# A two-layer hybrid decoder trunk whose instruction order is worked out against another machine model

## The chip, the core and the metric

The kernel runs on one core of a Trainium2 chip. The core has a matrix engine (PE, with its weight loads listed apart as PEld), a vector engine (DVE), a scalar engine (ACT), a general-purpose engine (POOL), a sync engine (SP) that here only issues transfers, and 16 DMA engines that move data between main memory and the on-chip memory. Each engine works through its own instruction list strictly in the order in which the program holds it, and waits on semaphores for the others. The metric is the device time of one execution in microseconds (us); less is better.

## What is computed

Two layers over x of 1024 tokens by 1024 channels, float32. Each layer has a mixer and an MLP, each between two norms:

```python
for l in range(2):
    z = rms_norm(x, g_pre_mix) @ w_in          # columns of three head groups
    # mLSTM, 4 heads of 64, chunks of 128, after a causal convolution and silu
    # sliding-window attention, 8 query heads on 2 key heads of 64, window 128, sinks
    # differential attention, 4 heads, 2 x 32 wide queries and keys, full causal
    x = x + rms_norm(concat(out_m, out_s, out_d) @ w_out, g_post_mix)
    u = square(relu(rms_norm(x, g_pre_mlp) @ w_up))     # 4096 wide
    x = x + rms_norm(u @ w_down, g_post_mlp)
```

## The kernel before, in words

All big products keep nearly float32 precision by splitting each operand into a high and a low part and adding three products: high by high, high by low, low by high. `load_w` (L103 to L118) brings a weight block in chunks by a DMA on SP's queue (L109) and splits it with one ACT and one DVE instruction per piece; `split` (L93, L94) does the same for activations.

A layer runs through these steps, written one after the other in the program:

- `p_d` (in `proj_tiles`, matmuls at L285, PSUM tile `pt`): the projections of the differential attention's queries and keys, with rotary embedding on DVE, stored to main memory as `d_rope` (L318, SP's queue). `p_g2` (L356, tile `pg`): gates and values.
- `e_diff`: the differential attention, 16 steps, each in four parts. `diff_load` loads `ks` and `qs` (L452 to L465, SP's queue). `diff1` makes a score tile `sp` per chunk (L493), reduces it on DVE with the mask (L496), takes the exponential on ACT (L499) and joins the two maps. `diff2` transposes (L520, tile `trd`), splits and multiplies with the values (L528, tile `pv`). `diff3` and `diff4` normalise and transpose back (L538, L555), and the result goes to main memory as `mix_d` (L558).
- `p_s`, `p_m` (L285, `pt`) and `p_g1` (L356, `pn`): the projections of the other two head groups. The key and query parts go to main memory as `s_ropek` (stores at L336) and `s_ropeq` (L318). The order is `p_s`, `p_g1`, `p_m` in layer 0 and `p_m`, `p_s`, `p_g1` in layer 1.
- `e_swa` and `e_mlstm`, interleaved by `run`: window attention (scores at L611, tile `ss`) and the mLSTM recurrence (L762 to L815).
- `out_group`, twice (L848, tile `po`), the second with `post_mix`: output projection, norm, residual, and the transpose for the MLP (L173, tile `tr`).
- The MLP: eight rounds of `up` (L1012, tile `pu`) and `down_mm` (L1057, tile `pd`), the last with `post_mlp`.

The program text is not the order of execution. Every instruction gets a priority number as it is written down, counting up. `ahead(n)` lowers the numbers inside its block by n, so that what stands there counts as that much earlier: `EARLY` (100000) for evacuations of `out_group` and `g2`, 5000 for the first loads, 1000 for weight loads and evacuations of projections, 300 or 200 for the window attention. When the `TileContext` block closes (L1198), the library's scheduler plays the program through on a model of the core. Whenever the model lets an engine take an instruction, the scheduler hands it the one with the lowest number among those whose inputs, by the model's clock, are finished and whose output buffer is free. The order so found is what each engine's list holds, DMA issues on SP's, ACT's and POOL's queues too. Buffers are handed out on the way: a pool has a fixed count per tag, for instance two PSUM buffers for each of the tags `mm`, `ad` and `as`, four of `e` and two of `at` on chip. Semaphore waits are added afterwards and keep the result right under any order. On the chip nothing is reordered: an instruction that is not ready holds up all that stand behind it on its engine. (Only weight loads run beside the matmul ahead of them, as the column PEld of the profile shows.)

The score tiles `sp` of the differential attention take their PSUM buffers from the tag `ad` (`diff1` calls with k of 0 or 1); the transposes and later parts of the first 11 steps take theirs from `as`:

```python
def dtag(k, h, g):
    return "as" if h * 4 + g < 11 and k >= 2 else "ad"
```

## Time and profile before

| | |
|---|---|
| Median of 3 runs | 2559.37 us (2557.65 to 2565.87) |
| The profiled execution, its own time | 2563.38 us |
| Its span, first to last instruction | 2561.6 us |
| Mean granted PE clock | 0.972 |
| Instructions | 32491 |
| Moved by DMA | 227.42 MB, 89 GB/s over the span |
| Matmul lines L1012 and L1057 (MLP) | 25.6% and 24.9% of the chain that ended last |

How to read the profile: busy time is the time in which an engine has an instruction recorded; the "granted clock" is the share of full speed that PE was given; a row of a list of groups names the line, engine, tile and shape, the count, the busy time, the mean duration of one, and the idle time of the engine just before them with what ended it. In a timeline a row is one instruction, or several alike in a run, with its start and its length; matmuls overlap in the records, so the distance from start to start is the pace, not the length. "SPq" is a DMA issue on SP's queue. The chain of waits goes back from the last instruction, at each step to what released it.

### The profile page before, as it was taken

The numbers are of one execution on the slowest core, as the hardware profiler recorded it, in microseconds if no ns is written. First come the engines' busy times: TensorE is split into PE (matmuls) and PEld (weight loads), VectorE is DVE, ScalarE is ACT, GpSimd is POOL, SyncE is SP. The second block draws the span as 40 slices with busy tenths as digits, with TensorE's granted clock in tenths as the row PEclk, the third lists the DMA queues.
The fourth block names the chain that finished last, engine by engine and source line by source line (L and its number), as shares of the span: only waits on it lengthen the run. The fifth ranks groups of instructions, "written<-read, shape, count | busy, mean of one in ns | idle before, by whom it ended". The sixth has DMA issues, their size and how long they took to land.

```text
span 2561.6 us, 32491 instructions
## 1 busy us (share of the span) xinstructions
PE 2397.5 (94%) x11556; PEld 1991.8 (78%) x11556; DVE 1457.8 (57%) x3604; ACT 1076.1 (42%) x2657; POOL 90.8 (4%) x174
## 2 busy tenths in 40 slices
PE   8888989889999999999999998878899999999998
PEld 7767867667888888888778777867678888888887
DVE  6676888775234434443675876867742344334436
ACT  4244777656313312331433645756553123213312
POOL 0000000010000000000000000000100000000000
PEclk9998999999999999999999989989999999999999
DMA  5444354333012101110442334433321112112204
GB/s 169 146 141 132 92 125 121 100 103 107 25 41 66 59 24 50 66 50 25 173 163 86 117 126 132 137 87 106 113 90 41 34 58 66 32 36 66 66 22 160
DMA packets 146002, 227.42 MB, mean 89 GB/s; under 512 B 22512, under 2 KB 60592, under 8 KB 145840
## 3 DMA queue, kind: packets, MB, share of 16 engines
q1 hardware_dynamic: 143680, 221.70, 28.1%
q10 hardware_dynamic: 2160, 3.65, 0.4%
q8 instruction: 91, 1.49, 0.2%
q14 instruction: 71, 0.58, 0.1%
HBM read 179.09 MB, written 46.20 MB: 88 GB/s over the span
## 4 chain that ended last, share of the span: by engine, by line
PE 73%; DMA 11%; DVE 7%; ACT 4%; issue 2%; POOL 1%; SPq 1%; DVEq 0%; POOLq 0%; ACTq 0%
PE pu L1012 26%; PE pd L1057 25%; PE pt L285 7%; PE po L848 2%; PE pg L356 2%; PE pn L356 2%; POOL rs L153 1%; DMA mb<-m_rows 1%; DMA qs<-d_rope 1%; PE pv L528 1%; DMA mix_d<-oo 1%; PE sp L493 1%; DMA mxl<-mix_d 1%; DMA rw<-in_w_t_dram 1%; PE ss L611 1%
## 5 line engine op out<-in xcount | busy, mean ns | idle before, releaser
L1012 PE MATMUL pu<-h2T,wu 128*128 128x512 f32 x3072 | 703.6, 390 | 0.1
L1012 PEld LDWEIGHTS pu<-h2T,wu 128*128 128x128 f32 x3072 | 577.4, 188 | 121.2 <-DVE h2T L94 1.1
L1057 PE MATMUL pd<-wdh,u 128*128 128x512 f32 x2048 | 635.2, 390 | 1.1 <-DVE acm L1068 1.1
L1057 PEld LDWEIGHTS pd<-wdh,u 128*128 128x128 f32 x2048 | 384.8, 188 | 81.1 <-DVE acm L1068 1.5
L1057 PE MATMUL pd<-wdl,u 128*128 128x512 f32 x1024 | 399.0, 390 | 0.0
L1068 DVE TENSOR_TENSOR acm<-acm,pd 128x512 f32<-128x512 f32 x224 | 153.1, 686 | 309.1 <-PE pd L1057 309.0
L1015 ACT ACTIVATE r<-pu 128x512 f32<-128x512 f32 x128 | 75.2, 588 | 537.9 <-PE pu L1012 537.9
L285 PE MATMUL pt<-hT,wt 128*128 128x512 f32 x832 | 287.2, 411 | 2.7 <-DVE lamp L228 1.5
L116 ACT ACTIVATE wu<-rw,gk 128x128 fp32r<-128x128 f32 x512 | 160.2, 390 | 184.7 <-PE pu L1012 132.3
L117 DVE SCALAR_TENSOR_TENSOR wu<-rw,gk,wu 128x128 fp32r<-128x128 f32 x512 | 154.2, 351 | 140.9 <-ACT wu L116 140.8
L1057 PEld LDWEIGHTS pd<-wdl,u 128*128 128x128 f32 x1024 | 192.6, 188 | 39.8
L1018 DVE TENSOR_TENSOR r<-r 128x512 f32<-128x512 f32 x128 | 88.4, 690 | 222.5 <-ACT u L1017 222.5
L285 PEld LDWEIGHTS pt<-hT,wt 128*128 128x128 f32 x832 | 160.5, 196 | 33.6 <-issue 2.3
L285 PE MATMUL pt<-lT,wt 128*128 128x512 f32 x416 | 170.2, 409 | 0.0
L153 POOL TENSOR_TENSOR rs<-ms,mhalf 128x1 f32<-128x1 f32 (+2 forms) x112 | 78.9, 709 | 2351.8 <-DVE ms L151 2283.2
L94 DVE TENSOR_TENSOR wdl<-rw,wdh 128x512 fp32r<-128x512 f32 x128 | 88.5, 692 | 105.1 <-ACT wdh L93 105.0
L848 PE MATMUL po<-woh,mxl 128*128 128x512 f32 x384 | 135.1, 410 | 10.4 <-DVE acc L856 7.8
L93 ACT CAST wdh<-rw 128x512 fp32r<-128x512 f32 x128 | 79.3, 620 | 129.2 <-DMA rw<-in_w_down_dram 129.2
L499 ACT ACTIVATE e<-e,nb 128x256 f32<-128x256 f32 (+7 forms) x128 | 99.4, 777 | 52.4 <-DVE nb L496 47.1
L493 PE MATMUL sp<-ks,qs 96*128 96x512 f32 (+2 forms) x192 | 74.0, 396 | 41.0 <-DMA qs<-d_rope 17.0
L356 PE MATMUL pn<-wv,hT 128*128 128x256 f32 x512 | 110.0, 296 | 0.2 <-ACT mv L707 0.2
L496 DVE CUSTOM_DVE_ANT_0 e<-sp,mdif 128x512 f32<-128x512 f32 (+3 forms) x128 | 74.5, 585 | 33.1 <-PE sp L493 24.0
(225 smaller groups left out, 3361.0 us busy)
## 6 DMA issues: line engine op xcount, KB each, us to landing
rw<-in_w_up_dram SPq DMA_DIRECT2D x128, 256.0 KB
rw<-in_w_down_dram SPq DMA_DIRECT2D x128, 256.0 KB
rw<-in_w_t_dram SPq DMA_DIRECT2D x52, 256.0 KB
tab<-in_rope_dram SPq DMA_DIRECT2D x20, 512.0 KB
xt<-in_x_dram SPq DMA_DIRECT2D x16, 512.0 KB
d_rope<-rot SPq DMA_DIRECT2D x32, 256.0 KB
s_ropeq<-rot SPq DMA_DIRECT2D x32, 256.0 KB
qq<-s_ropeq SPq DMA_DIRECT2D x16, 512.0 KB
```

The lines of the kernel that those rows point to most:

```text
L94: nc.vector.tensor_sub(lo, src, hi.bitcast(F32))
L116: nc.scalar.activation(hi[:, cs], rj, AF.Copy, scale=g)
L117: nc.vector.scalar_tensor_tensor(out=lo[:, cs], in0=rj, scalar=g, in1=hi[:, cs].bitcast(F32), op0=ALU.mult, op1=ALU.subtract)
L153: nc.gpsimd.tensor_tensor(out=rs, in0=ms, in1=mhalf[:, 0:n], op=ALU.pow)
L285: nc.tensor.matmul(q, lhsT=a, rhs=b, start=n == 0, stop=n == 23)
L356: nc.tensor.matmul(q[:, 0:n], lhsT=a, rhs=b, start=i == 0, stop=i == 23)
L493: nc.tensor.matmul(sp[:, 0:w], lhsT=qs[0:96, m, (q % 4) * P:(q % 4 + 1) * P], rhs=ks[m][0:96, c0:c0 + w], start=True, stop=True)
L499: nc.scalar.activation(e[:, 0:L], e[:, 0:L], AF.Exp, bias=nb[:, nch - 1:nch], scale=-1.0, accum_out=den[:, m:m + 1])
L848: nc.tensor.matmul(q, lhsT=mx[:, a, k], rhs=wo[k][b][:, n * 512:(n + 1) * 512], start=i == 0, stop=i == 3 * nk - 1)
L1012: nc.tensor.matmul(q, lhsT=w[:, a, kc], rhs=h2[b + half][:, :, kc], start=n == 0, stop=n == 23)
L1057: nc.tensor.matmul(q, lhsT=U[f][a][:, t * P:(t + 1) * P], rhs=D[f][b][:, n * 512:(n + 1) * 512], start=i == 0, stop=i == 3 * nf - 1)
L1068: nc.vector.tensor_add(a, a, q)
```

## The change

One argument is added where the kernel opens the `TileContext`. The scheduler then plays the program through on the library's detailed simulator of the core in place of its usual, simpler one. The priority numbers, the pools, the instructions and what they compute are the same; what can come out differently is the order of the instructions on each engine, DMA issues among them, and which instance of a pool's buffers a tile gets.

```diff
-    with tile.TileContext(nc) as tc:
+    with tile.TileContext(nc, schedule_with_timeline_sim=True) as tc:
         hybrid_kernel(tc, *args)
```

## The prediction

> **What bounds the kernel now.** I read the page first, then busy time by stretches, the chain of waits, PE's own waits, and last the timeline of one stall.

> ```profile
> span 2561.6 us, 32491 instructions
> PE 2397.5 (94%) x11556; PEld 1991.8 (78%) x11556; DVE 1457.8 (57%) x3604; ACT 1076.1 (42%) x2657; POOL 90.8 (4%) x174
> PE   8888989889999999999999998878899999999998
> PEclk9998999999999999999999989989999999999999
> ```

> PE is busy for 94% of the span, but the digits show that it isn't so evenly. Cutting the span where the chain shows the first and last unbroken MLP matmuls gives five stretches (columns: length; busy time of PE, PEld, DVE, ACT, POOL, each with its count; granted clock; DMA share; GB/s):

> ```profile
> 0.00:593.53 593.53, 512.13 (x2755) 427.28 (x2755) 429.75 (x1221) 336.65 (x868) 41.05 (x81) 0.94 0.43 126
> 593.53:1216.08 622.55, 622.55 (x2741) 515.22 (x2742) 253.57 (x505) 181.06 (x423) 0.00 (x0) 1.00 0.15 49
> 1216.08:1867.36 651.28, 576.18 (x3040) 481.26 (x3039) 474.07 (x1297) 355.82 (x906) 45.01 (x85) 0.95 0.41 124
> 1867.36:2532.28 664.92, 664.92 (x2929) 550.37 (x2930) 279.68 (x550) 196.81 (x452) 1.99 (x3) 1.00 0.17 54
> 2532.28:2561.60 29.32, 21.73 (x96) 17.65 (x95) 20.77 (x35) 5.76 (x10) 2.75 (x5) 0.95 0.54 189
> ```

> The two MLP stretches, 622.55 + 664.92 = 1287.5 us, have no PE idle time at all and full clock. The chain of waits runs through them matmul by matmul (start, length, what):

> ```profile
> 593.53 34.26 PE pu L1012 x144
> 627.79 43.52 PE pd L1057 x192
> 1867.36 33.86 PE pu L1012 x144
> ```

> 192 matmuls take 43.52 us, 0.227 us each. An order can't make these shorter. All that can move lies in the other 1274.1 us: the two mixers with their borders, and the tail. PE is busy there for 512.13 + 576.18 + 21.73 = 1110.0 us and idle for 164.1 us. What ended its longest idle times (total, times, longest):

> ```profile
> PE sp L493 <- DMA qs<-d_rope: 17.0, 3, 7.0
> PE tr L173 <- DVE ms L151: 11.7, 1, 11.7
> PE tr L173 <- ACT acc L166: 11.0, 15, 2.3
> PE po L848 <- DVE acc L856: 7.8, 3, 4.9
> PE sp L493 <- DMA ks<-d_rope: 7.7, 2, 4.9
> ```

> No cause dominates: the largest is 17.0 us, and most of the 164 us is small waits for DVE and ACT results. One of the stalls shows what an order does. First PE, then SP's queue:

> ```profile
> 131.70 0.48 PE L285 MATMUL pt<-hT,wt 128*128 128x512 f32 x1
> 137.69 0.98 PE L493 MATMUL sp<-ks,qs 96*128 96x512 f32 x2 [5.51 <-DMA qs<-d_rope]
> 138.68 0.63 PE L285 MATMUL pt<-hT,wt 128*128 128x512 f32 x1
> 139.10 0.63 PE L285 MATMUL pt<-lT,wt 128*128 128x512 f32 x1
> ...
> 144.21 0.28 PE L493 MATMUL sp<-ks,qs 96*128 96x256 f32 x1
> 144.33 0.40 PE L285 MATMUL pt<-lT,wt 128*128 128x512 f32 x1
> 144.56 0.40 PE L285 MATMUL pt<-hT,wt 128*128 128x512 f32 x1
> 144.79 0.39 PE L493 MATMUL sp<-ks,qs 96*128 96x512 f32 x1
> 145.03 0.39 PE L285 MATMUL pt<-hT,wt 128*128 128x512 f32 x1
> 145.26 0.39 PE L285 MATMUL pt<-lT,wt 128*128 128x512 f32 x1
> 145.49 0.28 PE L493 MATMUL sp<-ks,qs 96*128 96x256 f32 x1
> ```

> ```profile
> 119.62 0.63 SPq L464 DMA_DIRECT2D qs<-d_rope  x1
> 123.68 2.66 SPq L336 DMA_DIRECT2D s_ropek<-rot  x4
> 126.39 1.36 SPq L465 DMA_DIRECT2D qs<-d_rope  x1
> ```

> A score matmul stood at the head of PE's list while its query load was on the way, and `pt` matmuls that needed nothing stood behind it. The second half of that load had itself been put behind four `s_ropek` stores on SP's queue. It was issued at 126.39 and PE went on at 137.69, 11.3 us later. Behind the stall the pace is 0.42 us a matmul (138.68 to 139.10) against 0.23 us (144.33 to 144.56): after such a gap PE runs at half clock for a while. The rows from 144.21 on show how the attention rides on filler: two `pt` matmuls between one score matmul and the next.

> **The change part by part.** Nothing is added to or taken from the instructions, so every sum is one of places.

> *MLP stretches: 0.* What hides a moved weight load, split or evacuation there is PE itself: DVE is busy 253.57 of 622.55 us and ACT 181.06. If that cover went, a PSUM evacuation late by more than a group of 24 matmuls (24 x 0.227 = 5.4 us) would stall PE. DVE at 41% and ACT at 29% leave that far off.

> *What can be gained in the rest.* Of the 164.1 us idle, 11.7 us (first row on `ms`) is the wait for the first data and 29.32 - 21.73 = 7.6 us is the last tail; neither moves. 145 us is left. To this comes the clock: (1 - 0.94) x 593.5 + (1 - 0.95) x 651.3 = 68 us of full speed not granted. So 213 us is the bound of the gain, and 2346 us that of the time. It can't be near: the small waits are for results of a dependent chain (score, reduction, exponential, transpose, product), and no list makes a result come sooner when there is no filler to put ahead. What a better notion of when transfers land could take is the 17.0 + 7.7 = 24.7 us on `qs` and `ks`, with a share of the clock loss.

> *What can be lost.* The attention is a chain of turns through few buffers, and its speed hangs on how soon PE takes a ready score matmul. The counts and the stretch of layer 0 in which they run (first and last window of 32 us that hold any; PE's share of this tile alone):

> ```profile
> L493 PE MATMUL sp<-ks,qs 96*128 96x512 f32 x96 | 42.4, 442 | 21.2 <-DMA qs<-d_rope 12.5 <-DVE ms L151 3.9 <-issue 3.7
> L493 PE MATMUL sp<-ks,qs 96*128 96x256 f32 x64 | 21.2, 342 | 19.5 <-DMA ks<-d_rope 7.7 <-DVE nb L496 5.6 <-DMA qs<-d_rope 4.5
> L493 PE MATMUL sp<-ks,qs 96*128 96x384 f32 x32 | 11.5, 365 | 0.3 <-DVE on L547 0.3
> ```

> ```profile
> 96.00:128.00 32.00, 3.08 (x8) 0.89 0.42 127
> 320.00:352.00 32.00, 3.35 (x8) 1.00 0.24 76
> ```

> That is 192 score tiles, 96 a layer, which run in layer 0 between 96 and 352 us, some 250 us: 2.6 us a tile. They go through two PSUM buffers, so a pair takes 5.2 us a round, of which the matmul's own 0.34 to 0.44 us is little. If each score matmul comes k filler matmuls later, each round of a pair grows by k x 0.227 us: 48 x 0.227 x k = 10.9 k us a layer, 21.8 k in both. The filler isn't lost, since PE has done it sooner, but the work that follows is no longer waiting on PE alone; I take half as given back, 10.9 k in all. The ends for k: 0, and below 0 if the new order is quicker to take a score. I take k = 3, by the timeline above: 2 to 3 filler matmuls is the spacing now, so this is a score matmul that misses its place and gets the next one. That gives 33 us.

> Why later rather than sooner: a model that charges for more of what an instruction passes through on its way (issue, queues, landing) sees each result of the chain later than a simpler one, and hands PE filler in the meantime; and it has more to delay (192 score tiles, and the transposes and products behind them) than to save (5 stalls on loads).

> *SP's, ACT's and POOL's queues.* Each load and store can take another place. The trio of SP rows above prices a bad one: 119.62 to 126.39, 6.8 us, between two halves of a load. A good one takes this away and the 5.51 us with it. I leave them at 0, with both ends among the cases. POOL's 90.8 us of small steps lie under DVE and PE work; its order has one candidate at a time.

> A check from the other side: the kernel holds the same mixer in two orders, since layer 1 runs its parts in another sequence.

> ```profile
> 11.73 1.97 PE L173 MATMUL tr<-mk,xt 128*128 128x128 f32 x8 [11.73 <-DVE ms L151]
> 1290.39 0.39 PE L285 MATMUL pt<-hT,wt 128*128 128x512 f32 x1
> ```

> Layer 0 takes 593.53 - 11.73 = 581.8 us and layer 1 takes 1867.36 - 1290.39 = 577.0 us. Two sequences of the same parts lie 4.8 us apart. So the mixer doesn't swing wildly, and tens of us for both layers is a fit size, not hundreds.

> **Sum.** The span of 2561.6 us plus 0 (MLP) plus 33 us gives 2594.6; the profiled execution took 2563.38, 1.8 more than its span, and the runs' median, 2559.37, lies 4.0 below that. So 2559.4 + 33 = 2592 us. k from 1 to 7 gives +11 to +76: this case's own range is 2570 to 2640.

> [...]

> **The rivals.** *Loads are seen rightly (faster).* The detailed model lands `qs` and `ks` as late as the chip does, PE gets `pt` matmuls ahead of the five blocked heads, and SP's loads go ahead of stores. It saves 24.7 us, and of the clock loss a like share, 24.7 / 164.1 x 68 = 10 us: 2559.4 - 35 = 2524 us; with a third of the other 120 us of movable waits (145 - 24.7) as well it would be 2484. For it: the stall above, where ready work stood behind. [...] It decides where the saving on loads outweighs k = 3, that is, if k stays under 3 while the five stalls go.

> *A deep queue is modelled (much slower).* If the model lets PE take some 10 matmuls before they run, each urgent one joins behind all of them, 2.3 us later: 10.9 x 10 = 109 us, 2668 us. For it: the filler to queue up is there, as the `pt` rows between the scores show. Against: once the filler is used up, the queue is empty and the delay ends. [...]

> *The orders come out nearly alike, or the argument does little.* Urgent instructions still go first by their numbers and PE has the same filler; the 4.8 us between two sequences speaks for it. 2559 us.

> **Chances.** Moderately slower 0.40; much slower 0.12; alike 0.12; faster 0.36. A measurement of this kernel can tell about 0.3% (7.7 us) from no change, so: faster 0.36, same 0.12, slower 0.52. The range runs from 2510, leaving out a tenth at the far end of the faster case, to 2675, leaving out a tenth above the deep queue.

> **What would show it.** Right: the MLP stretches keep their length and full PE; the attention's scores are spread over more than 250 us a layer, with more `pt` or `pn` between two of them; PE's wait on `qs` and `ks` shrinks or stays, and the mixers grow from 581.8 and 577.0 us by about 16 each. Wrong: idle PE time inside the MLP; mixers shorter than 570 us, with the waits on loads gone; or lists in which the same instructions stand at the same places.

## The result and the profile after

The changed kernel takes 2668.32 us (median of 4 runs, 2667.28 to 2669.36), against 2559.03 us for the kernel before in the same job: a ratio of 1.0422, 95% interval 1.0402 to 1.0441. It is 109 us slower. The sign of the forecast was right; the size, 33 us, was a third of what came.

The head of the page of after, to set beside the one of before:

```profile
span 2665.5 us, 32516 instructions
PE 2442.2 (92%) x11556; PEld 2029.6 (76%) x11556; DVE 1459.2 (55%) x3604; ACT 1078.2 (40%) x2657; POOL 92.4 (3%) x174
PE   8878978789999999999988978787799999999998
PEclk9989978999999999999998989688999999999999
```

The same matmuls (x11556) cost 44.7 us more of busy time, though nothing of them has changed. The slices that fell are those of the two mixers. Busy time by stretches, cut at the same landmarks of the chain as before (length; busy time of PE, PEld, DVE, ACT, POOL with counts; granted clock; DMA share; GB/s):

```profile
0.00:638.74 638.74, 533.05 (x2765) 444.88 (x2766) 433.66 (x1225) 336.97 (x869) 42.19 (x81) 0.92 0.39 117
638.74:1257.46 618.72, 618.19 (x2727) 511.55 (x2727) 249.06 (x498) 179.58 (x418) 0.00 (x0) 1.00 0.15 49
1257.46:1974.07 716.61, 607.06 (x3051) 507.55 (x3051) 480.81 (x1301) 360.13 (x910) 45.45 (x85) 0.90 0.37 113
1974.07:2636.33 662.26, 662.18 (x2922) 547.99 (x2921) 275.67 (x547) 195.76 (x450) 2.02 (x3) 1.00 0.17 54
2636.33:2665.50 29.17, 21.75 (x96) 17.66 (x95) 20.00 (x34) 5.75 (x10) 2.74 (x5) 0.93 0.54 189
```

The MLP stretches are full as before, and 3.8 and 2.7 us shorter, which only says that the cuts fall a few matmuls apart. The mixers grew by 45.2 and 65.3 us. Of these 110.5 us PE was idle for 58.7 more ((638.74 - 533.05) - 81.4 = 24.3, and (716.61 - 607.06) - 75.1 = 34.4) and busy for 51.8 more (20.9 + 30.9): the granted clock fell from 0.94 to 0.92 and from 0.95 to 0.90, and the same matmuls ran longer. Some 5 of the 51.8 us are only the cuts: 10 and 11 more matmuls fall on the mixers' side, at 0.227 us each.

PE's own waits of after (total, times, longest):

```profile
PE sp L493 <- DVE nb L496: 29.0, 25, 5.1
PE sp L493 <- DMA qs<-d_rope: 18.0, 3, 10.0
PE sp L493 <- DMA ks<-d_rope: 4.1, 1, 4.1
```

The waits on `qs` and `ks` did not go away: 22.1 us, where before had 24.7. New is the size of the first row. It says that a score matmul stood at the head of PE's list while its PSUM buffer was still being read by the reduction at L496. In before the same row is

```profile
PE sp L493 <- DVE nb L496: 6.5, 3, 5.1
```

Of the 25 waits of after, 19 (15.5 of the 29.0 us) lie behind the last filler matmul of their layer: score matmuls waiting for a turn, with no filler left to put in between.

Where the filler went, the timeline of PE shows. Two score matmuls of layer 0, and what stands between them:

```profile
321.81 0.40 PE L493 MATMUL sp<-ks,qs 96*128 96x512 f32 x1
322.05 0.40 PE L285 MATMUL pt<-hT,wt 128*128 128x512 f32 x1
322.28 0.40 PE L285 MATMUL pt<-lT,wt 128*128 128x512 f32 x1
322.52 0.62 PE L285 MATMUL pt<-hT,wt 128*128 128x512 f32 x2
322.97 0.39 PE L285 MATMUL pt<-lT,wt 128*128 128x512 f32 x1
323.20 0.61 PE L285 MATMUL pt<-hT,wt 128*128 128x512 f32 x2
323.65 0.39 PE L285 MATMUL pt<-lT,wt 128*128 128x512 f32 x1
323.88 0.61 PE L285 MATMUL pt<-hT,wt 128*128 128x512 f32 x2
324.33 0.28 PE L528 MATMUL pv<-at,v6d 128*128 128x256 f32 x1
324.45 0.29 PE L493 MATMUL sp<-ks,qs 96*128 96x256 f32 x1
```

Ten `pt` matmuls, where the rows of before had two. Soon after, the filler has been used up. Rows from the same view, with others left out at the dots:

```profile
329.94 0.75 PE L493 MATMUL sp<-ks,qs 96*128 96x512 f32 x1 [1.49 <-DVE nb L496]
...
330.91 0.63 PE L285 MATMUL pt<-hT,wt 128*128 128x512 f32 x1
331.41 0.58 PE L493 MATMUL sp<-ks,qs 96*128 96x256 f32 x1
...
335.72 1.12 PE L520 MATMUL trd<-mk,e 128*128 128x128 f32 x4 [3.73 <-ACT oo L557]
...
349.95 0.50 PE L493 MATMUL sp<-ks,qs 96*128 96x512 f32 x1 [3.00 <-DVE nb L496]
```

The row at 330.91 is the last `pt` matmul of layer 0. The attention itself isn't done, as the rows of the tile `sp` in layer 0 say (count; min, median and longest in ns; first and last start; forms), before first and after below:

```profile
L493 PE MATMUL sp<-ks,qs x96: 279/396/767, 101.2 to 338.8; 96*128 96x512 f32 x48, 96*128 96x256 f32 x32, 96*128 96x384 f32 x16
```

```profile
L493 PE MATMUL sp<-ks,qs x96: 280/396/795, 104.7 to 415.7; 96*128 96x512 f32 x48, 96*128 96x256 f32 x32, 96*128 96x384 f32 x16
```

238 us became 311, and in layer 1 274 became 368. In before the last `pt` ran 35 us after the last score; in after it ran 85 us before it. What is left of the attention then runs alone, and the clock falls with it. The window of 64 us in which that happens, before first:

```profile
320.00:384.00 64.00, 54.15 (x275) 42.75 (x273) 51.75 (x137) 46.87 (x118) 6.20 (x19) 0.95 0.52 124
```

```profile
320.00:384.00 64.00, 45.48 (x185) 33.87 (x183) 46.33 (x147) 41.36 (x119) 4.08 (x9) 0.71 0.32 90
```

185 matmuls in place of 275, at a granted clock of 0.71 in place of 0.95.

Counted in the order in which PE runs them, the mean run of filler (`pt` and `pn`) between two other matmuls in layer 0's attention is 4.5 in before and 9.2 in after; 35 of the 96 score matmuls stand behind the last filler, where before has none.

### The profile page after: what moved, and what is told of

The parts are those of the page before. It is cut to its first block, busy times and chain, and to the rows that moved or that the text cites. A ratio compares the mean times of both kernels' runs of the same rounds, so it can differ in the third digit from the quotient of the medians.

```text
span 2665.5 us, 32516 instructions
## 1 busy us (share of the span) xinstructions
PE 2442.2 (92%) x11556; PEld 2029.6 (76%) x11556; DVE 1459.2 (55%) x3604; ACT 1078.2 (40%) x2657; POOL 92.4 (3%) x174
## 4 chain that ended last, share of the span: by engine, by line
PE 70%; DMA 14%; DVE 10%; ACT 3%; issue 2%; SPq 1%; POOL 1%; DVEq 0%; POOLq 0%; ACTq 0%
PE pu L1012 25%; PE pd L1057 24%; PE pt L285 6%; DMA mb<-m_rows 5%; PE po L848 4%; PE pn L356 2%; PE pg L356 2%; DMA rw<-in_w_t_dram 2%; DMA d_rope<-rot 1%; DMA s_ropeq<-rot 1%; PE pv L528 1%; DMA s_ropek<-rot 1%; PE trd L520 1%; DVE e L496 1%; DMA rw<-in_w_out_dram 1%
## 5 line engine op out<-in xcount | busy, mean ns | idle before, releaser
L1012 PE MATMUL pu<-h2T,wu 128*128 128x512 f32 x3072 | 703.9, 389 | 1.0 <-ACT r L1015 0.5
L1012 PEld LDWEIGHTS pu<-h2T,wu 128*128 128x128 f32 x3072 | 575.8, 188 | 122.1 <-ACT r L1015 1.5
L1057 PE MATMUL pd<-wdh,u 128*128 128x512 f32 x2048 | 636.1, 389 | 1.6 <-DVE acm L1068 1.6
L1057 PEld LDWEIGHTS pd<-wdh,u 128*128 128x128 f32 x2048 | 384.2, 188 | 81.6 <-DVE acm L1068 2.0
L1057 PE MATMUL pd<-wdl,u 128*128 128x512 f32 x1024 | 398.5, 389 | 0.0
L285 PE MATMUL pt<-hT,wt 128*128 128x512 f32 x832 | 279.0, 409 | 15.3 <-DVE t L315 6.6
L1015 ACT ACTIVATE r<-pu 128x512 f32<-128x512 f32 x128 | 75.1, 588 | 534.9 <-PE pu L1012 534.7
L1057 PEld LDWEIGHTS pd<-wdl,u 128*128 128x128 f32 x1024 | 192.2, 188 | 39.9
L285 PEld LDWEIGHTS pt<-hT,wt 128*128 128x128 f32 x832 | 161.0, 196 | 52.1 <-DVE t L315 6.7
L285 PE MATMUL pt<-lT,wt 128*128 128x512 f32 x416 | 169.0, 406 | 2.8 <-DVE lT L94 2.8
L499 ACT ACTIVATE e<-e,nb 128x256 f32<-128x256 f32 (+7 forms) x128 | 99.3, 776 | 112.7 <-DVE nb L496 110.5
L848 PE MATMUL po<-woh,mxl 128*128 128x512 f32 x384 | 137.5, 415 | 6.2 <-ACT woh L93 5.8
L493 PE MATMUL sp<-ks,qs 96*128 96x512 f32 (+2 forms) x192 | 82.3, 442 | 60.9 <-DVE nb L496 29.0
L356 PEld LDWEIGHTS pn<-wv,hT 128*128 128x128 f32 x512 | 86.3, 201 | 19.3 <-ACT wv L93 17.8
```

What stands on the lines that cost most here:

```text
L285: nc.tensor.matmul(q, lhsT=a, rhs=b, start=n == 0, stop=n == 23)
L356: nc.tensor.matmul(q[:, 0:n], lhsT=a, rhs=b, start=i == 0, stop=i == 23)
L493: nc.tensor.matmul(sp[:, 0:w], lhsT=qs[0:96, m, (q % 4) * P:(q % 4 + 1) * P], rhs=ks[m][0:96, c0:c0 + w], start=True, stop=True)
L499: nc.scalar.activation(e[:, 0:L], e[:, 0:L], AF.Exp, bias=nb[:, nch - 1:nch], scale=-1.0, accum_out=den[:, m:m + 1])
L848: nc.tensor.matmul(q, lhsT=mx[:, a, k], rhs=wo[k][b][:, n * 512:(n + 1) * 512], start=i == 0, stop=i == 3 * nk - 1)
L1012: nc.tensor.matmul(q, lhsT=w[:, a, kc], rhs=h2[b + half][:, :, kc], start=n == 0, stop=n == 23)
```

## The experiments

**PE's window, four sizes.** The first run sets it to 2, with one line ahead of the `TileContext`:

```diff
+    from concourse.hw_specs import TRN2Spec
+    TRN2Spec.ENG_ISSUE_QUEUE_DEPTH[mybir.EngineType.PE] = 2
     with tile.TileContext(nc, schedule_with_timeline_sim=True) as tc:
```

> As the changed kernel, but the detailed model's issue window of PE (how many instructions the model lets PE's sequencer take before the first of them is finished) is set to 2 instead of 35. In the instruction lists, filler matmuls between attention matmuls then come in runs of 4.8 instead of 9.2 (4.5 before). Theory A (the window decides: an urgent matmul joins behind whatever filler PE has already taken): most of the 109 us come back, 2550 to 2590 us. Theory B (the model's durations and latencies of single instructions decide, not the window): it stays near 2668 us, at least above 2640. Theory C (the windows of DVE, ACT and POOL decide): stays near 2668.

Measured: 2594.71 us, ratio to before 1.0142 (1.0118 to 1.0166): most of the loss is back, though 5 us less of it than A had said. Then 16 and 70, the same line with the other number:

> As the changed kernel with PE's window in the model at 16 instead of 35; runs of filler 6.4 in the list. Theory A: between the changed kernel and window 2, about 2600 to 2630 us. B and C: near 2668 us.

Measured: 2615.11 us, 1.0229 (1.0205 to 1.0253).

> As the changed kernel with PE's window in the model doubled to 70; runs of filler 13.1 in the list. Theory A: slower than the changed kernel, by half again to twice its loss, 2710 to 2780 us. B and C: near 2668 us.

Measured: 2720.17 us, 1.0636 (1.0616 to 1.0656). Beside the length of the filler runs, counted as above:

| PE's window | time, us | filler between other matmuls | scores behind the last filler |
|---|---|---|---|
| 2 | 2594.7 | 4.8 | 1 |
| 16 | 2615.1 | 6.4 | 18 |
| 35 (as given) | 2668.3 | 9.2 | 35 |
| 70 | 2720.2 | 13.1 | 48 |

Time, filler and leftover scores rise together: from window 2 on 20.4 us for 1.6 more filler matmuls, 73.6 for 4.4, 125.5 for 8.3, so 13 to 17 us for each. A holds for 74 of the 109 us. At window 2 the filler runs of layer 0 are nearly as short as in before (in layer 1 they are 5.3, before 4.4, with 8 scores behind the last filler), yet 36 us are left: something else is at work as well.

**The other engines' windows.** ACT, DVE and POOL from 12 to 2, PE at 35:

```diff
+    for e in ("Activation", "DVE", "Pool"):
+        TRN2Spec.ENG_ISSUE_QUEUE_DEPTH[getattr(mybir.EngineType, e)] = 2
```

> As the changed kernel, PE's window left at 35, but those of ACT, DVE and POOL in the model set to 2 instead of 12. Theory A: near 2668 us, within 20. Theory B: near 2668. Theory C (urgent vector and scalar steps join behind others already taken): most of the loss comes back, below 2600 us.

Measured: 2677.73 us, 1.0466 (1.0446 to 1.0486). C falls: 9 us slower than after, with filler runs of 9.5.

**The priority numbers.** The attention is made as urgent as the early evacuations:

```diff
-        run((e_diff(), 19, 0))
+        run((e_diff(), 19, EARLY))
```

> As the changed kernel, but the differential attention's priority numbers are lowered by 100000 (run((e_diff(), 19, EARLY))), so that nothing else can go ahead of it by number. Theory A: the numbers already put it ahead of all filler, and what is taken into the window cannot be overtaken: 2668 within 20 us. Rival N (other work with lower numbers, weight loads and evacuations at 1000, holds the attention up): most of the loss comes back, below 2620.

Measured: 2685.99 us, 1.0494 (1.0471 to 1.0518), 18 us slower than after, and the filler runs stay at 9.2. N falls, and this fits A: a lower number would be of no use to a score matmul that isn't ready when the choice is made.

**The landing of loads, alone and with the window.** A reason in the traces for D is one of DVE's waits for a load, in before, after and window 2:

```profile
DVE mb L757 <- DMA mb<-m_rows: 2.0, 1, 2.0
```

```profile
DVE mb L757 <- DMA mb<-m_rows: 77.4, 16, 6.7
```

```profile
DVE mb L757 <- DMA mb<-m_rows: 79.9, 16, 6.9
```

`m_rows` is the mLSTM's row of gates, loaded at L747 and added at L757 (a second load of it, L754, goes to ACT at L755). In after the add is put into DVE's list so early that all 16 of them block its head, with all else that DVE has to do behind them. One, on SP's queue and on DVE:

```profile
462.72 0.54 SPq L747 DMA_DIRECT2D mb<-m_rows  x1
```

```profile
467.31 0.42 DVE L769 TENSOR_TENSOR mb<-kn,ws 128x256 f32<-128x256 f32 x1
471.54 0.69 DVE L757 TENSOR_TENSOR mb<-mb,mk 128x512 f32<-128x512 f32 x1 [3.81 <-DMA mb<-m_rows]
472.15 0.68 DVE L94 TENSOR_TENSOR sb<-trs,sb 128x512 fp32r<-128x512 f32 x1
```

Issued at 462.72 and used at 471.54, 8.8 us: the list had counted on it sooner. So three kernels with later landing: the detailed model with window 2 and 4.35 us added on SP, the same with window 35, and the usual estimate with 4.0 us added.

```diff
+    TRN2Spec.DGE_DMA_DELAY[mybir.EngineType.SP] = 5000      # 650; detailed model
```

```diff
+    TRN2Spec.DMA_START_FIXED_NS = 5300.0                    # 1300; usual estimate
     with tile.TileContext(nc) as tc:
```

> As e1 (PE's window in the model 2), and every transfer from SP's queue starts 4.35 us later in the model (5.0 instead of 0.65 us), so that the scheduler sees loads land later. What is left of the loss in e1 is about 36 us. Theory D (the rest comes from loads that the detailed model lands too early: PE waits 35.2 us on qs in e1, 17.0 before): PE's wait on qs and ks falls below 10 us, and the time to 2545 to 2575 us. Theory E (the rest comes from the model's times of compute instructions, PE's waits for DVE being 102 us in e1 against 66 before): the waits on loads fall too, but waits for DVE take their place; 2585 to 2600 us.

Measured: 2517.14 us, 0.9827 (0.9808 to 0.9846): 1.7% faster than before, and 28 us below what D had said.

> As the changed kernel (window 35), with the same 4.35 us on every transfer of SP's queue in the model. Theory A (the window carries two thirds of the loss): stays above 2630 us. Theory D: up to 20 us less than the changed kernel, 2645 to 2665. If landing times were the main cause: below 2600.

Measured: 2590.82 us, 1.0113 (1.0096 to 1.0131). This is far below what A and D had said, in the range named for landing as the main cause.

> The kernel before, with its usual estimate, but a transfer's fixed start-up in that estimate 4.0 us longer (5.3 instead of 1.3 us). Theory D: the usual estimate also lands loads too early (24.7 us of PE's waits on qs and ks); 2530 to 2555 us, faster than before. Theory E: no gain, 2555 to 2580.

Measured: 2518.32 us, 0.983 (0.9807 to 0.9854), 12 us below what D had said. The wait rows of the three, in this order:

```profile
DVE mb L757 <- DMA mb<-m_rows: 32.5, 12, 5.5
PE sp L493 <- DMA qs<-d_rope: 7.1, 3, 3.3
```

```profile
PE sp L493 <- DVE nb L496: 24.6, 25, 4.1
DVE mb L757 <- DMA mb<-m_rows: 22.7, 13, 3.7
PE sp L493 <- DMA qs<-d_rope: 7.8, 2, 7.1
```

```profile
DVE mb L757 <- DMA mb<-m_rows: 7.8, 3, 3.3
PE sp L493 <- DMA qs<-d_rope: 4.3, 2, 2.2
```

Window and landing add up. Window 35 to 2 saves 73.6 us with the given landing (2668.3 to 2594.7) and 73.7 with the later one (2590.8 to 2517.1); the later landing saves 77.6 us at window 2 and 77.5 at window 35. (These runs are of three jobs; by their ratios to before the steps are 0.0280 and 0.0286, and 0.0315 and 0.0309.) The row `PE sp <- DVE nb` stays with the wide window whatever the landing (24.6 us in 25 waits, the second fence), the row on `m_rows` shrinks with the landing. And with window 2 and later landings, the detailed model and the usual estimate give the same time, 2517 and 2518 us; E would have kept them apart.

So from after either setting alone brings back about 75 us, and the two together 151, which is 42 more than the change lost. The 36 us that window 2 leaves are within what landing moves (77.6), but no run gives both models the same landing, so that landing is all of the 36 isn't shown.

**How far landing can be turned.** In the usual estimate, from 1300 ns to 0 and to 9300:

> The kernel before, with its usual estimate, but a transfer's fixed start-up in it 0 instead of 1.3 us, so that loads land sooner in the estimate. Theory D (the sooner the model lands loads, the worse the order): slower than before by 10 to 40 us, 2570 to 2600. If landing times matter only above some point already passed: 2555 to 2568.

Measured: 2653.86 us, 1.0379 (1.0348 to 1.0409), over 50 us above the 2570 to 2600 that were expected. Its filler runs are as in before (4.7) and DVE's row on `m_rows` is only 10.9 us, so an early landing costs in other places too; which ones wasn't taken apart.

> The kernel before, with its usual estimate, but the fixed start-up of a transfer 9.3 instead of 1.3 us (5.3 gave 2518 us). Theory D with the chip's own landing times of some 8 to 11 us as the best value: 2495 to 2515 us. If 5.3 us already covers most loads: 2515 to 2545, since what is put off too far leaves gaps of its own.

Measured: 2632.99 us, 1.0301 (1.0272 to 1.0329); expected was a gain. Both say that the time is more sensitive to this one figure than either theory had it: 0, 1.3, 5.3 and 9.3 us give 2654, 2557, 2518 and 2633 us (the second the kernel before in this job). The last of them loses in other places, by its rows of PE's waits (the third is 11.0 us in 15 waits in before):

```profile
PE pd L1057 <- ACT wdh L93: 23.0, 33, 1.2
PE pd L1057 <- DVE wdl L94: 12.9, 55, 0.5
PE tr L173 <- ACT acc L166: 37.2, 11, 6.0
```

The MLP, which had no idle time in before, now waits for the splitting of its weights (35.9 us), and nearly all of the third row lies where an MLP begins. The mixers are short there (the MLP's first `pu` starts at 550.2 us, in before at 574.2).

**Is it the blocked heads on DVE?** The add at L757 moves to POOL, which has time (92.4 us busy), once at window 35 and once at window 2:

```diff
-            nc.vector.tensor_add(rb, rb, m_st.unsqueeze(1).broadcast_to([P, 4, P]))
+            nc.gpsimd.tensor_add(rb, rb, m_st.unsqueeze(1).broadcast_to([P, 4, P]))
```

> As e1 (PE's window 2; 2595 us), with the 16 additions of L757 on POOL. Theory F: the rest of the loss goes, 2555 to 2572 us. Rival G: 2585 us or more.

Measured: 2566.39 us, 1.0038 (1.0024 to 1.0052): 28 of the 36 us that window 2 had left are gone (27 by the ratios). POOL does most of the waiting now, and DVE a part of it one line earlier, at L756, behind ACT's exponential of the second load:

```profile
POOL mb L757 <- DMA mb<-m_rows: 131.3, 13, 21.3
DVE mb L756 <- ACT mb L755: 25.7, 6, 6.6
```

> As the changed kernel (window 35), but the 16 additions of L757 that wait for the m_rows loads run on POOL instead of DVE. In the changed kernel DVE stood 77.4 us before them, at all 16; before the change 2.0 us. Theory F (the part of the loss that isn't the window's, some 36 us, sits in these 16 blocked heads of DVE's list): 2630 to 2645 us. Rival G (DVE's standing there is idle time that costs nothing, and the early landing costs elsewhere): within 12 us of 2668.

Measured: 2665.72 us, 1.0429 (1.0405 to 1.0454), no gain at all. But the move freed DVE only in part here:

```profile
DVE mb L756 <- ACT mb L755: 44.8, 10, 7.0
ACT mb L755 <- DMA mb<-m_rows: 60.1, 10, 8.6
```

In after L756 never waited for ACT. So 44.8 of the 77.4 us moved one line up DVE's list and stayed, and ACT waits as it did (51.9 us in after). What went from DVE, 33 us, brought nothing; what the blocked heads as a whole cost with the wide window isn't settled by this run. The landing is worth 77.5 us there too (from after to the window 35 kernel with later landing). That kernel's scores take 275 us in layer 0 (to 391.5 us, after's to 415.7) and 325 in layer 1, against 311 and 368 in after, so with the wide window the gain shows in the attention. Which of the loads brings it there wasn't taken apart.

## Why the prediction was right or wrong

*MLP stretches, 0.* Right: 0.5 and 0.1 us of idle time, a granted clock of 1.00, the same length but for the cuts.

*"If each score matmul comes k filler matmuls later".* The mechanism was right. The filler runs grew, the scores of a layer were spread over 311 and 368 us where over 250 was named, the filler was used up before the attention, and each step of the window's size moves the time with the length of the runs.

*"I take k = 3" and "I take half as given back".* These are the steps that failed in size. By the filler runs k is 9.2 - 4.5 = 4.7, not 3 (the runs are counted between all other matmuls, so they don't tell scores from the transposes and products behind them). And from window 2 to 35 the runs grow by 4.4, which at the prediction's full price of 21.8 us each is 96 us; measured are 74, so three quarters stayed, not half. The argument for giving back was that filler done sooner isn't lost. It is not lost, but the rows behind 330.91 show what it was worth: the attention needed it as cover to the end, and without it PE was idle for 18.5 of the 64 us from 320 to 384 and was granted a clock of 0.71 there. The term was 74 us and not 33. The k of 3 was read off the spacing that there was, on the thought that a late matmul misses one place; how many it misses is set by how far ahead the model has chosen.

*"I leave them at 0" (SP's, ACT's and POOL's queues).* Wrong, by some 36 us (what window 2 leaves, of which 28 go with one add), and for a reason that the prediction had only as a gain: when the model lands loads *sooner* than the estimate did, instructions that depend on them are put too early. The prediction looked for this on PE alone, at `qs` and `ks`, 24.7 us. It grew most on DVE, where before showed a single wait of 2.0 us on `m_rows`. But the sign was there, on ACT, for the same tensor and larger than the 24.7 us:

```profile
ACT mb L755 <- DMA mb<-m_rows: 32.8, 7, 8.6
```

In after it is 51.9 us, and in the usual estimate with later landing 2.1. DVE (77.4 us in after) and ACT have lists too, with heads that block.

*"A model that charges for more … sees each result of the chain later".* Not what the runs show. With the window at 2, the detailed model's filler runs are nearly those of the usual estimate (4.8 to 4.5), though all its other charges stand; and its loads seem to land sooner, not later, since PE's wait on `qs` is 35.2 us there against 17.0 in before, and DVE's on `m_rows` 79.9 against 2.0.

*The rival "loads are seen rightly".* The kernel did not do it: the detailed model's landings were too early still. But its mechanism is real and was priced a little low: with 5.3 us in place of 1.3, the usual estimate gains 44 us, where 35 were worked out. The waits on `qs` shrink to 4.3 us, as that rival had it. Landing as late as the traces have it is not the best value, though: with 9.3 us the kernel loses 76.

*The rival "a deep queue is modelled".* Its number, 2668, is the result, partly by chance: it took 10 matmuls at half price, and what came was 4.7 at three quarters and 36 us of landing. Its cause, the window, is right for the larger part. It was given 0.12 because "once the filler is used up, the queue is empty and the delay ends", which was taken as the end of the loss and is its beginning. At a window of 70 the lists have 13.1 - 4.5 = 8.6, still short of those 10. The window is a setting of the model, and no run here shows whether, or how far, the chip's PE takes instructions ahead.

*The check "Two sequences of the same parts lie 4.8 us apart".* It misled. It compared two orders that the same model had made, both with short filler runs, and so said nothing of an order made by other rules.

*What stays open:* at window 35, which loads bring the landing's 77.5 us, and what the blocked heads on DVE and ACT cost; where a landing of 0 loses its 96 us; and whether the 8 us that remain at window 2 with the add on POOL (2566.4 against 2557.5) are all landing.

## What to carry to other kernels

An order that is chosen ahead of results spends filler where urgent work would soon have been ready, so look in the instruction lists how long the filler runs are and whether the filler lasts to the end of the chain that it covers. A list on an in-order engine is as good as its notion of when loads land: look for single instructions that wait for a load at the head of any engine, DVE and ACT included (here 77.4 and 51.9 us on `m_rows`), and try the planner's landing time at several values. Moving this one figure from 1.3 to 5.3 us beat both kernels and mattered more than the choice of simulator (2518 us with the usual one, 2517 with the detailed one at window 2 and a later landing), while 0 and 9.3 us cost 96 and 76 us, though the traces have loads of 8.8 and 11.3 us: the best value was found by trial, not read from the trace. When a blocked instruction is moved to another engine, look at what now stands at the head of the list it left.

## What the runs showed of the hardware

Loads took 8.8 us (`m_rows`, 462.72 to 471.54) and 11.3 us (`qs`, in the prediction) from issue to use, with a DMA share of 0.38 and 0.28 in those two windows; no run tells what made them this long. Behind the second, after PE's 5.51 us of idle time, the granted clock was 0.50 from 137.69 to 141.00. And the clock was part of the price of sparse work: with the filler gone PE was granted 0.71 in the window shown above and, in layer 1,

```profile
1664.00:1728.00 64.00, 47.12 (x189) 35.12 (x189) 48.62 (x171) 39.31 (x119) 5.51 (x10) 0.65 0.23 63
```

0.65. The same score matmul lasted longer where the clock was lower. Its rows in 320 to 384 us (count; busy time; mean ns of one; idle time before), before and after:

```profile
L493 PE MATMUL sp<-ks,qs 96*128 96x512 f32 x6 | 2.5, 415 | 0.0
L493 PE MATMUL sp<-ks,qs 96*128 96x512 f32 x13 | 8.0, 623 | 5.9 <-DVE nb L496 5.9
```

So some 47 of the mixers' 110.5 us came to stand in the busy column. The clock fell by a factor of 1.34 in this window (0.95 to 0.71) and these records grew by 1.50, so that the clock is all of it isn't shown.
